# Five second-matmul products of a Strassen MLP get a second level, grown in PSUM

## The chip, the cores and the metric

The kernel runs on 1 core of a Trainium2 chip. The metric is device time in microseconds (us), lower is better. TensorE multiplies into PSUM (8 banks of 128x512 f32), VectorE, ScalarE and GpSimd work beside it, and SyncE (SP) and GpSimd issue the DMAs, each on a queue of its own. Below, one "superblock" is 1024 of the 8192 tokens.

## The reference

```python
# x (8, 1024, 1024), w1 (1024, 4096), w2 (4096, 1024), all float32
h = x @ w1
h = 0.5 * h * (1 + np.tanh(np.sqrt(2 / np.pi) * (h + 0.044715 * h ** 3)))
return (h @ w2).astype(np.float32)
```

## The kernel before

**Tiling.** The 8192 tokens are worked in 8 superblocks of 1024, one after the other; each has a matmul 1 (x by w1, with the gelu) and a matmul 2 (by w2). Operands are float16, sums in PSUM are float32. Both matmuls are split by Strassen's method in Winograd's form: every matrix is cut into four blocks (11, 12, 21, 22), and seven products of sums of blocks take the place of eight products of blocks. The tables `W_SUM` and `S_SUM` (L19, L21) say how an operand sum is made: sum 5 of w2 is block 12 minus block 11, sum 6 is block 22 minus sum 5, and so on; `W_TERM` and `S_TERM` (L18, L20) name the products that take a plain block. The order of the products of matmul 2 in superblocks 0 and 1 is 1, 2, 5, 6, 3, 7, 4.

**One level and two.** A product can itself be done by seven smaller products ("second level", here called steps). Superblocks 0 and 1 run `matmul1` (matmuls L485) and `matmul2_made`, whose products have one level: for each of four token quarters `q`, `matmuls2` (L1059) issues 16 matmuls of 128x512 into one PSUM bank, so 64 in a product. Superblocks 2 to 7 run `matmul1_late` (L699) and `matmul2` (L1018), whose seven products have two levels: 7 steps of 16 matmuls of 128x256, so 112 in a product. The second level needs sums of quarters of both operands. Those of w2 ("inner sums") are made once, by the jobs of `split_jobs`, and stored to the DRAM tensors `in_d[m]`, from which superblocks 2 to 7 load them; the sums of w2 blocks themselves are stored to `w2_d`.

**What happens after a bank.** `post` takes the finished bank of a product and quarter: ScalarE copies it to a temporary (products 1, 5, 6) or VectorE adds it to one (2, 3, 7), and finished outputs are stored over GpSimd's queue. Products that share a letter in the list of `matmul2_made` grow in the same banks ("a", "b", "c").

**Order.** Matmuls, copies, sums and the DMAs issued by `load_in_order` (L158, on SP's queue) keep the order in which the program writes them, engine by engine; each engine takes its queue in that order and stands at an instruction whose data or buffer isn't there. What VectorE does between the products is written by hand in `FILL` (L44 to L58), one table for each of superblocks 0 and 1. The key `61` means after product 6, quarter 1. Its jobs: `g` a sum of gelu outputs (the matmul 2 operand that stands still in TensorE), `w51` piece 1 of w2's sum 5, `p57` the inner sum 7 of product 5's w2 operand, `x`, `q` and `i` sums of the next superblock's x and w1. VectorE's sums all go through `tt` (L135), ScalarE's copies through `act_copy` (L162).

**Memory.** w2 blocks, their sums, inner sums, x blocks and x sums are tiles of the pool `up` (26 buffers, named `u`); stationary sums are tiles of `gcp` (4, named `gc`), float32 temporaries of `tp` (10, `tmp`), PSUM tiles of `pp` (8, `ps`). In `matmul2_made`, `bring` fetches the four pieces of a w2 block (and casts them, in superblock 0), `keep` stores them (superblock 0 only), `x_transpose` fetches the next superblock's x over SP's queue.

Of the kernel before, what the change touches and what calls it, by code (L numbers as in the profile page):

```python
# [14 lines left out]
P = 128  # L15
# [24 lines left out]
def slots(table):  # L40
    return {(int(k[0]), int(k[1])): v.split() for k, v in (row.split(":") for row in table.split(";"))}


FILL = (  # L44
    slots("""10:g60 p15;11:g61 p16;12:g62 p17;13:g63
    ;20:g50 w50 w51;21:g51 w52;22:w53 g52;23:g53 p14
    ;50:w60 w61;51:w62 w63;52:g30 g31;53:g32 g33
    ;60:w70 w71;61:w72 w73;62:w40 w41;63:w42 w43
    ;73:x5;40:x7 x6;41:x3 q5;42:q6 q7 q4
    ;43:i2 i3 i1 i5""".replace("\n    ", "")),  # L50
    slots("""10:g60 w50;11:g61 w51;12:g62 w52;13:g63 w53
    ;20:g50 p55;21:g51 p56;22:g52 p57;23:g53 p54
    ;50:w60 w61;51:w62 w63;52:g30 g31;53:g32 g33
    ;60:p65 w70;61:p66 w71;62:p67 w72;63:p64 w73
    ;30:w40 w41;31:w42 w43;32:p75;33:p76
    ;70:p77 p74;71:x5 p45;72:x7 p46;73:x6 p47
    ;40:p44;41:x3;42:i2;43:i3""".replace("\n    ", "")),
)  # L58
# [13 lines left out]
def kernel(  # L72
# [192 lines left out]
    class StoredHalf:  # L265


        def __init__(self, i, room=()):
            q, h = divmod(i, 2)
            self.ops, self.sums = {}, {}  # L270
            self.room = list(room)
            for ks in GROUPS:
                two = None
                if ks != ("s1", "s5"):
                    two = self.two(ks)
                    if ks == (1, 5):
                        self.both = two
                elif 0 < i < MADE_HALF:
                    two = self.two(ks)
                if two is not None:  # L280
                    nc.sync.dma_start(
                        out=two[:, :len(ks)].rearrange("p e n -> p (e n)"),
                        in_=w1_d[q, ks][:, h].rearrange("p e n -> p (e n)"),
                    )
# [233 lines left out]

    def matmul1(xs, sb, quads, start=None):
        g = g_tiles()  # L520
# [25 lines left out]
        for j in range(NI // 2):  # L546
# [62 lines left out]
            if end:  # L609
                six(0)  # L610
                gelu("11", cs[0], a[0])
                six(1)
                gelu("11", cs[1], a[1])
                for h in range(2):
                    five(h)
# [190 lines left out]

    def matmul2_made(sb, g, keep_w1, xb):

# [30 lines left out]
        def make(m, q):  # L839
            if m not in sums:  # L840
                sums[m] = raw[over[m]] if m in over else [unit(2, HALF) for _ in range(NI // QC)]
            u, op, v = W_SUM[m]
            in0, in1 = (sums[b][q] if isinstance(b, int) else raw[b][q] for b in (u, v))
            tt(sums[m][q], in0, in1, op, True)
            if sb:
                n = 1 if q < 2 else 2
                nc.gpsimd.dma_start(out=w2_at(q, m)[:, :n], in_=sums[m][q][:, :n])

        def pieces(m):
# [4 lines left out]

        s2, a, p5, t6, at = {}, {}, {}, {}, {}
        operands = {1: "11", 2: "12", 4: "22", 7: "21", 5: "11", 3: "12"}
        splits = {m: split_jobs(m, lambda m=m: pieces(m)) for m in (1, *SUMS)}

        def run(key):
            for job in FILL[sb].get(key, ()):  # L860
                kind, m, n = job[0], int(job[1]), int(job[2:] or 0)
                if kind == "g" and m == 6:
                    s2[n] = gcp.tile([P, NI, P], GT, name="gc")
                    tt(s2[n], rows(g["22"], n), rows(g["21"], n), SUB, True)
                elif kind == "g" and m == 5:
                    tt(rows(g["11"], n), s2[n], rows(g["11"], n), ADD, True)
                elif kind == "g":
                    tt(rows(g["12"], n), rows(g["12"], n), s2[n], SUB, True)
                elif kind == "w":
                    make(m, n)  # L870
                elif kind == "p":
                    splits[m][SUMS.index(n)]()
                elif kind == "x":
                    xs.make(m, pin=True)
                elif kind == "q":
                    quad.sum(m, pin=True)
                elif kind == "i" and sb:
                    xs.make_inner(m)
                elif kind == "i":
                    quad.inner_sums(m)  # L880

        def post(m, q, bank):
            if m in (1, 5, 6):
                t = {1: a, 5: p5, 6: t6}[m]
                t[q] = temp()
                act_copy(t[q], bank)
            elif m == 4:
                c = temp()
                act_copy(c, bank)
                store(sb, "21", q, c)  # L890
            else:
                t = {2: a, 3: t6, 7: p5}[m][q]
                tt(t, t, bank, ADD, True)
                at[q] = store(sb, {2: "11", 3: "12", 7: "22"}[m], q, t)

        bring("11", pool_copy, False)
        bring("21", pool_copy, False)
        bring("12", act_copy, True)
        keep("11")
        if sb:  # L900
            bring("22", None, False)
        banks = {"a": [], "b": [], "c": []}
        for m, name, first in (
            (1, "a", True), (2, "b", True), (5, "c", True), (6, "a", False),
            (3, "c", False), (7, "a", False), (4, "a", False),
        ):
            for q in range(NQ):
                if first:
                    banks[name].append(psum())
                bank = banks[name][q]  # L910
                matmuls2(bank, s2[q] if m == 6 else rows(g[operands[m]], q), pieces(m), first)
                post(m, q, bank)
                if (m, q) == (5, 0) and sb == 0:
                    xb = x_cast(sb + 1, nc.gpsimd.tensor_copy(out=pace, in_=p5[0][:, :2]))
                if (m, q) == ((5, 0) if sb else (6, NQ - 1)):
                    xs = XOps(x_transpose(xb, load_in_order))
                    keep("22")
                if (m, q) == (3, NQ - 1) and sb == 0:
                    quad = MadeQuad(0, False, True)
                if (m, q) == (4, 0) and sb:  # L920
                    quad = StoredHalf(0)
                if (m, q) == (1, NQ - 1) and sb == 0:
                    sums[5] = [unit(2, HALF) for _ in range(NI // QC)]
                    for t in sums[5]:
                        act_copy(t[:, 0, :1], warm)
                    bring("22", act_copy, True)
                    keep("21")
                    keep("12")
                run((m, q))
        return xs, [quad]  # L930

    def split_jobs(m, pieces):
        t = {}

# [6 lines left out]
        def make(n):  # L941
            u, op, v = W_SUM[n]
            t[n] = unit(NI // 2, OH // 2)
            for h in range(2):
                tt(t[n][:, h * QC:(h + 1) * QC, :], operand(u, h), operand(v, h), op, True)
            nc.gpsimd.dma_start(out=in_d[m][:, SUMS.index(n)], in_=t[n])

        return [lambda n=n: make(n) for n in SUMS]

    def split_in_m1(m, h):  # L950

        raw, t = [], {}
        for k in range(2):
            raw.append(gcp.tile([P, 2, HALF], DT, name="gc"))
            q = 2 * k + h
            nc.sync.dma_start(out=raw[k], in_=w2_at(q, m))

# [200 lines left out]
    for sb in range(NSB):  # L1158
        if sb < 2:
            g, nxt = matmul1(xs, sb, quads, first if sb == 0 else None)  # L1160
            xs, quads = matmul2_made(sb, g, None if sb else quads[-1].keep_raw, nxt)
            continue
# [33 lines left out]
```

## Time and profile before

| | us |
|---|---|
| median of 3 runs | 1467.45 (1466.58 to 1467.8) |
| the profiled execution: its span (no other time of it is recorded; the median lies 2.55 above) | 1464.9 |
| matmul 2 of superblock 0 (111.94 to 208.63) | 96.69 |
| matmul 1 of superblock 1 (208.63 to 305.32) | 96.69 |
| matmul 2 of superblock 1 (305.32 to 402.01) | 96.69 |
| a later matmul 2 (492.76 to 578.35) | 85.59 |

The span is read from the hardware profile of one execution: first instruction to last. The times of the stages are those of TensorE's unbroken stretches in the chain of work that ended last, on the same clock. In the second matmuls of superblocks 0 and 1, VectorE was busy for 54.70 and 67.84 us, ScalarE for 26.93 and 10.43 and GpSimd for 17.78 and 26.72 (the table by stretches). Over the whole span the DMA engines moved 315 GB/s.

### The profile page before, as it was taken

Reading aid. Unit: us, or ns where it says so; the run is one execution under the profiler, and the core shown is the slowest. Engines: PE = TensorE matmul, PEld = TensorE weight load, DVE = VectorE, ACT = ScalarE, POOL = GpSimd, SP = SyncE. Lnnn points to the kernel's source line nnn. Section 1 sums busy time; section 2 is a strip of 40 time slices with the busy share of each in tenths; the row PEclk is TensorE's granted clock in tenths of the full one; section 3 lists DMA queues with packets and bytes.
Section 4 is the critical chain, followed back from the end, with each engine's and each line's share of the span. In section 5 each row is a group of like instructions: output and inputs, shape, how many; then the busy total and the mean of one; then the engine's idle time right before and its main releaser. Section 6 shows DMA issues by size and latency. Waiting matters only on the chain.

```text
span 1464.9 us, 27508 instructions
## 1 busy us (share of the span) xinstructions
PE 1456.8 (99%) x10383; PEld 1012.9 (69%) x10383; DVE 1166.0 (80%) x1940; ACT 600.7 (41%) x1226; POOL 443.6 (30%) x471
## 2 busy tenths in 40 slices
PE   8999999999999999999999999999999999999998
PEld 5444444444466788668876688767887678866787
DVE  6657459757677899879997799977998779887897
ACT  5665125631066411663126621366214652056410
POOL 1441123312347011560026501274103721136011
PEclk9999999999999999999999999999999999999999
DMA  9999899998998999979999899998999999996896
GB/s 330 342 349 392 229 342 360 385 300 230 353 323 215 360 276 366 375 207 373 307 369 338 203 373 326 359 305 248 350 346 347 297 280 313 352 367 215 310 302 206
DMA packets 207429, 462.15 MB, mean 315 GB/s; under 512 B 75840, under 2 KB 80960, under 8 KB 206400
## 3 DMA queue, kind: packets, MB, share of 16 engines
q1 hardware_dynamic: 179808, 364.96, 72.4%
q0 software_dynamic: 27488, 95.44, 21.9%
q8 instruction: 81, 1.33, 0.3%
q14 instruction: 52, 0.43, 0.1%
HBM read 361.76 MB, written 113.25 MB: 324 GB/s over the span
## 4 chain that ended last, share of the span: by engine, by line
PE 99%; DMA 1%; SPq 0%; DVE 0%; issue 0%; DVEq 0%
PE ps L1018 35%; PE ps L485 31%; PE ps L699 19%; PE ps L1059 13%; PE ps L418 1%; DMA gc<-in_w_dram 1%; SPq L159 0%; PE ps L395 0%; DVE u L223 0%; DVE u L135 0%; DVE u L406 0%; DVEq L135 0%
## 5 line engine op out<-in xcount | busy, mean ns | idle before, releaser
L485 PE MATMUL ps<-u 128*128 128x512 f16 x1808 | 423.5, 379 | 0.0
L135 DVE TENSOR_TENSOR tmp<-tmp,ps 128x512 f32<-128x512 f32 x498 | 280.3, 581 | 106.0 <-PE ps L485 44.6
L162 ACT COPY tmp<-ps 128x512 f32<-128x512 f32 (+1 forms) x398 | 209.4, 545 | 259.4 <-PE ps L1059 135.2
L135 DVE TENSOR_TENSOR ps<-tmp,ps 128x256 f32<-128x256 f32 x552 | 222.7, 425 | 102.9 <-PE ps L699 83.7
L1018 PE MATMUL ps<-u,gc 128*128 128x256 f16 x2688 | 300.3, 273 | 0.0
L485 PEld LDWEIGHTS <-u 128*128 128x128 f16 x1808 | 176.9, 98 | 170.2
L1018 PEld LDWEIGHTS <-gc 128*128 128x128 f16 x2688 | 263.0, 98 | 30.4
L699 PEld LDWEIGHTS <-u 128*128 128x128 f16 x2170 | 212.3, 98 | 67.9 <-issue 0.4
L498 ACT ACTIVATE g<-ps 128x512 f16<-128x512 f32 x326 | 192.9, 596 | 105.3 <-PE ps L699 64.9
L135 DVE TENSOR_TENSOR u<-u 128x2048 f16<-128x2048 f16 (+3 forms) x288 | 214.7, 787 | 23.6 <-DMA w_d<-u 10.9
L1018 PE MATMUL ps<-u,g 128*128 128x256 f16 x2016 | 227.9, 273 | 0.0
L162 ACT COPY u<-ps 128x512 f32<-128x512 f32 (+1 forms) x134 | 78.0, 587 | 354.9 <-PE ps L1018 348.0
L805 POOL DMA_DIRECT2D out_dram<-u x70 | 63.9, 936 | 498.2 <-DVE u L135 264.9
L1018 PEld LDWEIGHTS <-g 128*128 128x128 f16 x2016 | 197.2, 98 | 22.8
L699 PE MATMUL ps<-u 128*128 128x256 f16 x1298 | 193.6, 273 | 0.0
L135 DVE TENSOR_TENSOR u<-u,ps 128x512 f32<-128x512 f32 x216 | 147.7, 684 | 36.5 <-PE ps L1018 25.3
L1059 PE MATMUL ps<-u,g 128*128 128x512 f16 x768 | 166.4, 379 | 0.0
L498 ACT ACTIVATE g<-tmp 128x512 f16<-128x512 f32 x186 | 117.4, 633 | 99.0 <-DVE tmp L135 98.7
L306 POOL TENSOR_TENSOR u<-u 128x512 f16<-128x512 f16 x120 | 136.3, 1157 | 31.8 <-PE ps L699 22.4
L699 PE MATMUL ps<-gc,u 128*128 128x256 f16 x872 | 145.7, 273 | 0.0
L1059 PEld LDWEIGHTS <-g 128*128 128x128 f16 x768 | 75.1, 98 | 90.6
L1012 DVE TENSOR_TENSOR gc<-g,gc 128x2048 f16<-128x2048 f16 x84 | 102.4, 1220 | 3.1 <-PE ps L1018 3.1
(52 smaller groups left out, 854.8 us busy)
## 6 DMA issues: line engine op xcount, KB each, us to landing
u<-w_d SPq DMA_DIRECT2D x322, 512.0 KB, 9.1
u<-in_d SPq DMA_DIRECT2D x168, 512.0 KB, 7.9
out_dram<-u POOLq DMA_DIRECT2D x70, 512.0 KB, 10.8
gc<-in_w_dram SPq DMA_DIRECT2D x48, 512.0 KB, 6.0
g<-w_d SPq DMA_DIRECT2D x40, 512.0 KB, 12.0
w_d<-u POOLq DMA_DIRECT2D x36, 512.0 KB, 7.5
w_d<-u SPq DMA_DIRECT2D x32, 512.0 KB, 9.2
xb<-in_x_dram POOLq DMA_DIRECT2D x56, 256.0 KB, 6.8
```

Of the source, the lines that this page charges most:

```text
L135: i = nc.vector.tensor_tensor(out=out, in0=in0, in1=in1, op=op)
L162: tc.keep_in_program_order(nc.scalar.copy(out=out, in_=in_))
L306: nc.gpsimd.tensor_tensor(out=operand(j), in0=operand(u), in1=operand(v), op=op)
L418: tc.keep_in_program_order(nc.tensor.matmul(bank[:, cols], lhsT=w[:, k, :], rhs=self.xs.blocks[f"{a}{r}"][:, k, cols], start=r == 1 and k ...
L485: tc.keep_in_program_order(nc.tensor.matmul(bank, lhsT=w, rhs=x, start=first and k == 0, stop=k == n - 1, skip_group_check=not first,))
L498: gelu_last[0] = nc.scalar.activation(out=out, in_=src, func=GELU)
L699: tc.keep_in_program_order(nc.tensor.matmul(out, lhsT=w, rhs=x, start=first and k == 0, stop=k == 1, skip_group_check=not first,))
L805: return nc.gpsimd.dma_start(out=rows, in_=src, **kw)
L1012: tc.keep_in_program_order(engine.tensor_tensor(out=self.s[j], in0=in0, in1=in1, op=op))
L1018: tc.keep_in_program_order(nc.tensor.matmul(bank[:, i * OH // 2:(i + 1) * OH // 2], lhsT=t[:, c, i * P:(i + 1) * P], rhs=self.y[j][:, c, : ...
L1059: tc.keep_in_program_order(nc.tensor.matmul(pair(bank), lhsT=a[:, c, :], rhs=chunks(pieces[c // QC])[:, :, c % QC, :], start=(first and c ...
```

## The change

Product 4 of superblock 0 and products 1, 2, 7 and 4 of superblock 1 (the table `DEEP`) get a second level, by the new class `Deep`. It runs its seven steps in the order 1, 5, 6, 2, 7, 3, 4, each in two halves `i` of 128 tokens with 8 matmuls of 128x256, and adds up the steps inside PSUM. Of four banks, two ("upper", `bank(i)`) become the first two token quarters of the product and two ("low", `bank(2 + i)`) the last two. Step 1 goes into low left, and ScalarE copies that to upper left. Step 5 goes into low right, and ScalarE copies that to a temporary. Step 6 adds to low left, and VectorE puts the sum of temporary and low left into upper right. Step 2 adds to upper left. Step 7 adds to low left, and VectorE puts the sum of temporary and low left into low right. Step 3 adds to upper right, step 4 to low left, after which `post` takes the banks.

`Deep.make` (job kind `s` in `FILL`: `s75` is sum 5 for product 7) makes the stationary sums on VectorE, `Deep.load` fetches the stored inner sums over SP's queue. For product 1 of superblock 1 the sums are made by `tail`, called in the last part of that superblock's matmul 1. The `FILL` tables are rewritten: w2's sums 7 and 4 and their inner sums are made in superblock 0, stored over GpSimd's queue; superblock 1 makes sums 5 and 6 and theirs. Sums 5 and 6 are stored over SP's queue (`keep_sum`), as are the inner sums of 6 (`gate`), with the loads of products 2, 7 and 4 behind them on it. In superblock 1 block 12 is fetched before 21 and 22, and the transposes of x are issued after quarter 3 of product 5, not quarter 0. In superblock 0 the block 22 is stored one product earlier (after quarter 3 of product 5, not of 6), ahead of the transposes. Product 4 (and 7 where it is deep, in superblock 1) takes new banks and no longer grows in those of product 1: two float32 tiles of the pool `up` (`half_of`) collect output 21, from products 6, 7 and 4 in superblock 1 and from 7 and 4 in superblock 0. The load of the first stored half of a w1 quad (`StoredHalf(0)`) goes through `load_in_order`.

```diff
+DEEP = ((4,), (1, 2, 7, 4))
+SPLIT_IN_M2 = (7, 4)
+DEEP_STEPS = (1, 5, 6, 2, 7, 3, 4)
 FILL = (
     slots("""10:g60 p15;11:g61 p16;12:g62 p17;13:g63
     ;20:g50 w50 w51;21:g51 w52;22:w53 g52;23:g53 p14
     ;50:w60 w61;51:w62 w63;52:g30 g31;53:g32 g33
-    ;60:w70 w71;61:w72 w73;62:w40 w41;63:w42 w43
-    ;73:x5;40:x7 x6;41:x3 q5;42:q6 q7 q4
-    ;43:i2 i3 i1 i5""".replace("\n    ", "")),
-    slots("""10:g60 w50;11:g61 w51;12:g62 w52;13:g63 w53
-    ;20:g50 p55;21:g51 p56;22:g52 p57;23:g53 p54
+    ;60:w40 w41;61:w42 w43;62:p45 p46;63:p47 p44
+    ;30:w70 w71;31:w72 w73;32:p75 p76;33:p77 s45
+    ;70:p74;71:s47 x5;72:s46;73:s43 x7
+    ;40:x6;41:x3;42:q5;43:q6;44:q7;45:q4;46:i2 i3 i1 i5""".replace("\n    ", "")),
+    slots("""00:w50 w51 w52 w53
+    ;11:s25;12:s27;14:s26;15:s23
+    ;21:g60;22:g61 g50;23:g51;24:g62;25:g63 g52;26:g53
     ;50:w60 w61;51:w62 w63;52:g30 g31;53:g32 g33
-    ;60:p65 w70;61:p66 w71;62:p67 w72;63:p64 w73
-    ;30:w40 w41;31:w42 w43;32:p75;33:p76
-    ;70:p77 p74;71:x5 p45;72:x7 p46;73:x6 p47
-    ;40:p44;41:x3;42:i2;43:i3""".replace("\n    ", "")),
+    ;60:p55 p56;61:p57 p54;62:p65 p66;63:p67 p64
+    ;30:s75;31:s77;32:s76;33:s73
+    ;70:x5;71:x7;72:s45;73:x6;74:s47;75:x3;76:s46
+    ;40:s43;42:i2;43:i3""".replace("\n    ", "")),
 )
 ...
                 gelu("11", cs[1], a[1])
+                if tail is not None:
+                    tail(g)
 ...
+    class Deep:
+        def __init__(self, m, t, pieces, sums=None):
+            self.m, self.pieces = m, pieces
+            self.x, self.s = {b: inner_block(t, b) for b in BLOCKS}, {}
+            self.y = {} if sums is None else sums
+            self.banks, self.copies = {}, {}
+
+        def make(self, j):
+            u, op, v = S_SUM[j]
+            self.s[j] = gcp.tile([P, NI // 2, HT // 2], GT, name="gc")
+            in0, in1 = (self.s[t] if isinstance(t, int) else self.x[t] for t in (u, v))
+            tt(self.s[j], in0, in1, op, True)
+
+        def load(self, steps):
+            for j in steps:
+                self.y[j] = unit(NI // 2, OH // 2)
+                if j in W_TERM:
+                    k, b = (int(d) - 1 for d in W_TERM[j])
+                    load_in_order(
+                        self.y[j].rearrange("p c n -> p (c n)"),
+                        w2_d[k, self.m][:, b].rearrange("p h n -> p (h n)"),
+                    )
+                else:
+                    load_in_order(self.y[j], in_d[self.m][:, SUMS.index(j)])
+
 ...
+        def step(self, j, i):
+            h, cols = {5: (1, right), 2: (0, left), 3: (0, right)}.get(j, (1, left))
+            bank = self.bank(2 * h + i)
+            t = self.x[S_TERM[j]] if j in S_TERM else self.s[j]
+            for c in range(NI // 2):
+                tc.keep_in_program_order(nc.tensor.matmul(
+                    bank[:, cols],
+                    lhsT=t[:, c, i * P:(i + 1) * P],
+                    rhs=self.moving(j, c),
+                    start=(j == 1 and c == 0),
+                    stop=(c == NI // 2 - 1),
+                    skip_group_check=j != 1,
+                ))
+            low = self.banks[2 + i]
+            if j == 1:
+                act_copy(self.bank(i)[:, left], low[:, left])
+            elif j == 5:
+                if not self.copies:
+                    t = temp()
+                    self.copies.update({0: t[:, left], 1: t[:, right]})
+                act_copy(self.copies[i], low[:, right])
+            elif j == 6:
+                tt(self.bank(i)[:, right], self.copies[i], low[:, left], ADD, True)
+            elif j == 7:
+                tt(low[:, right], self.copies[i], low[:, left], ADD, True)
 ...
-            if sb:
+            if sb == 0 and m in SPLIT_IN_M2:
                 n = 1 if q < 2 else 2
                 nc.gpsimd.dma_start(out=w2_at(q, m)[:, :n], in_=sums[m][q][:, :n])
 
+        def keep_sum(m):
+            for q in range(NI // QC):
+                n = 1 if q < 2 else 2
+                load_in_order(w2_at(q, m)[:, :n], sums[m][q][:, :n])
 ...
+        def half_of(q):
+            if q % 2 not in v:
+                v[q % 2] = up.tile([P, 2, OH], F32, name="u")
+            return v[q % 2][:, q // 2, :]
 ...
+                if m == 6 and 7 in deep:
+                    act_copy(half_of(q), bank)
+            elif m == 7:
+                if m in deep:
+                    t = half_of(q)
+                    tt(t, t, bank, ADD, True)
+                    tt(p5[q], p5[q], t, ADD, True)
+                else:
+                    act_copy(half_of(q), bank)
+                    tt(p5[q], p5[q], bank, ADD, True)
+                store(sb, "22", q, p5[q])
             elif m == 4:
-                c = temp()
-                act_copy(c, bank)
-                store(sb, "21", q, c)
+                t = half_of(q)
+                tt(t, t, bank, ADD, True)
+                store(sb, "21", q, t)
             else:
-                t = {2: a, 3: t6, 7: p5}[m][q]
+                t = {2: a, 3: t6}[m][q]
                 tt(t, t, bank, ADD, True)
-                at[q] = store(sb, {2: "11", 3: "12", 7: "22"}[m], q, t)
+                at[q] = store(sb, {2: "11", 3: "12"}[m], q, t)
 
         bring("11", pool_copy, False)
-        bring("21", pool_copy, False)
-        bring("12", act_copy, True)
+        if sb:
+            bring("12", None, True)
+            deep[1].load((5, 6, 7, 4))
+            bring("21", None, False)
+            run((0, 0))
+            keep_sum(5)
+            deep[2].load((5, 6, 7, 4))
+            bring("22", None, False)
+        else:
+            bring("21", pool_copy, False)
+            bring("12", act_copy, True)
         keep("11")
-        if sb:
-            bring("22", None, False)
-        banks = {"a": [], "b": [], "c": []}
+        banks = {"a": [], "c": []}
+
+        def events(m, q):
+            nonlocal xs, xb, quad
+            if sb:
+                if (m, q) == (5, NQ - 1):
+                    keep_sum(6)
+                    deep[7].load(DEEP_STEPS)
+                    xs = XOps(x_transpose(xb, load_in_order))
+                elif (m, q) == (3, 0):
+                    deep[4].load(DEEP_STEPS)
 ...
+            if (m, q) == (5, NQ - 1) and sb == 0:
+                keep("22")
+            if (m, q) == (6, NQ - 1) and sb == 0:
+                xs = XOps(x_transpose(xb, load_in_order))
 ...
+            if (m, q) == (4, 0) and sb:
+                quad = StoredHalf(0, dma=load_in_order)
 ...
+            run((m, q))
+
+        xs = quad = None
         for m, name, first in (
-            (1, "a", True), (2, "b", True), (5, "c", True), (6, "a", False),
-            (3, "c", False), (7, "a", False), (4, "a", False),
+            (1, "a", True), (2, None, True), (5, "c", True), (6, "a", False),
+            (3, "c", False), (7, None if 7 in deep else "a", 7 in deep), (4, None, True),
         ):
+            if m in deep:
+                d = deep[m]
+                for n, j in enumerate(DEEP_STEPS):
+                    for i in range(2):
+                        d.step(j, i)
+                        if j in (3, 4):
+                            post(m, i if j == 3 else 2 + i, d.banks[i if j == 3 else 2 + i])
+                    events(m, n)
+                if name is not None:
+                    banks[name] = [d.banks[q] for q in range(NQ)]
+                continue
             for q in range(NQ):
 ...
-                if (m, q) == ((5, 0) if sb else (6, NQ - 1)):
-                    xs = XOps(x_transpose(xb, load_in_order))
-                    keep("22")
 ...
-            nc.gpsimd.dma_start(out=in_d[m][:, SUMS.index(n)], in_=t[n])
+            if gate:
+                load_in_order(in_d[m][:, SUMS.index(n)], t[n])
+            else:
+                nc.gpsimd.dma_start(out=in_d[m][:, SUMS.index(n)], in_=t[n])
 ...
+            early = []
+
+            def tail(g):
+                early.append(Deep(1, g["11"], None))
+                for n in (5, 7, 6, 3):
+                    early[0].make(n)
+
+            g, nxt = matmul1(xs, sb, quads, first if sb == 0 else None, tail if sb else None)
+            xs, quads = matmul2_made(sb, g, None if sb else quads[-1].keep_raw, nxt, *early)
```

## The prediction

> **What bounds the kernel now.** I read the page first (busy shares, then the chain), then the chain in order of time for the length of each stage, then TensorE's waits, then the single instructions on VectorE around the edited code.
>
> From the page, busy time by engine and the chain by engine:
>
> ```profile
> PE 1456.8 (99%) x10383; PEld 1012.9 (69%) x10383; DVE 1166.0 (80%) x1940; ACT 600.7 (41%) x1226; POOL 443.6 (30%) x471
> ...
> PE 99%; DMA 1%; SPq 0%; DVE 0%; issue 0%; DVEq 0%
> ```
>
> From the chain in order of time (start, length in us), a one-level second matmul (L1059) and a two-level one (L1018), whole:
>
> ```profile
> 305.32 96.69 PE ps L1059 x448
> ...
> 492.76 85.59 PE ps L1018 x784
> ```
>
> TensorE is the chain, without gaps. Seven one-level products take 96.69, so one takes 13.81 (64 matmuls of 0.216). Seven two-level products take 85.59, so one takes 12.23 (112 of 0.109). The two-level stage of the late superblocks runs unbroken, so its matmuls hide their weight loads. TensorE has no wait after the first 12 us. Whatever makes TensorE wait is therefore paid in full, and nothing later can win it back.
>
> VectorE, from its timeline (start, length): a 128x2048 f16 sum behind another, a pair of 128x1024 ones, an add at the end of matmul 1; then the page's row of a 128x256 add in PSUM:
>
> ```profile
> 301.10 0.69 DVE L135 TENSOR_TENSOR tmp<-tmp,ps 128x512 f32<-128x512 f32 x1 [3.01 <-ACT tmp L162]
> 302.82 1.88 DVE L135 TENSOR_TENSOR tmp<-tmp,ps 128x512 f32<-128x512 f32 x3 [1.04 <-PE ps L485]
> ...
> 306.72 1.23 DVE L135 TENSOR_TENSOR gc<-g,g 128x2048 f16<-128x2048 f16 x1
> 307.86 1.22 DVE L135 TENSOR_TENSOR u<-u 128x2048 f16<-128x2048 f16 x1
> ```
> ```profile
> 115.19 1.28 DVE L135 TENSOR_TENSOR u<-u 128x1024 f16<-128x1024 f16 x2
> 116.40 1.21 DVE L135 TENSOR_TENSOR gc<-g,g 128x2048 f16<-128x2048 f16 x1
> ```
> ```profile
> L135 DVE TENSOR_TENSOR ps<-tmp,ps 128x256 f32<-128x256 f32 x552 | 222.7, 425 | 102.9 <-PE ps L699 83.7
> ```
>
> Back to back, then: 1.14 for a 2048-wide sum (a "job" below), 0.605 for a 1024-wide one, 0.6 for a 512-wide add out of PSUM (three in 1.88), 0.43 for a 256-wide add. VectorE is busy 67.84 of the 96.7 us of superblock 1's second matmul (the table by stretches), so there is little room in it.
>
> VectorE also takes its queue in order, and stands still at a wait while later work is ready. Its waits from 140 to 215 us (total, times, longest):
>
> ```profile
> DVE u L135 <- DMA w_d<-u: 10.9, 3, 5.6
> ```
>
> Those were the `w7` sums of superblock 0, held by stores. TensorE did not notice, as no PSUM add that it needed stood behind them.
>
> **The gain.** Five products become two-level: 5 x (13.81 - 12.23) = **7.93 us** less on TensorE.
>
> **What a two-level product needs.** Seven steps of 1.75 us (two halves of 0.87): 1, 5, 6, 2, 7, 3, 4. After each half of 6, VectorE adds into the upper bank that step 2 writes next, so step 2 waits for the add. Only 6's other half (0.87) covers it, and the add takes 0.43: it is free if VectorE is idle at that moment, and every job ahead in its queue is paid by TensorE beyond about 0.4. The operand sums (`s` jobs) must be ready too. So I go through VectorE's queue product by product.
>
> *Superblock 0, product 4.* When product 7 ends, the queue is its last add (0.7), `s43`, `x7`, `x6`, `x3` (4 x 1.14), then the add of step 6: done at 5.8 to 6.2 after the product starts (the two ends use 1.14 and 1.25 a job). Step 2 was due at 5.24: **0.9 lost**. The loads and stores around it move (22 is now kept ahead of the transposes of x), but `x7` comes 8 us after the transposes landed before. Range 0.5 to 3.
>
> *End of matmul 1 in superblock 1.* The four sums of `tail` need the last gelu of g11, which ended at 299.8. Four jobs take VectorE from there to 304.4. The add of p5 that ran at 301.10 runs after them, until 305.1. The last two pieces of matmul 1 (`four`, 0.86 each) write the bank it reads, and were due at 305.2 - 1.7 = 303.5. **1.65 lost**; range 1 to 2.2.
>
> *Product 1.* ScalarE is still busy with the two last gelus 1.7 us into the product; its bank copy (0.38) holds step 5 for **0.35**. VectorE's queue: the g21 difference until 1.3, `w50` to `w53` until 5.85, `s25` until 7.0, then the add of step 6 until 7.4. Step 2 was due at 5.6: **1.8 lost**.
>
> *Product 2.* VectorE is just in time (`g60` ends 0.4 ahead of the add). Its own operands are loaded behind the four stores of sum 5, which wait for `w50` to `w53`: issued 6 to 12 us into product 1 (each also waits for the eighth DMA before it on SP's queue), the first is wanted at 16.2. A load of this kind landed after 9.2 at the median (DMA issues, 300 to 410 us), so 15.5 to 21. I take **0.5**; range 0 to 3.
>
> *Products 5, 6, 3* stay one-level, and their operands are made early enough.
>
> *Product 7 is the point of the change.* Four inner sums of sum 5 (`p55 p56 p57 p54`) stand in VectorE's queue during product 6, ahead of the four of sum 6, the adds of product 3 and the four `s` sums of product 7. Each makes a new tile of the pool `up`, which has 26. When `p57` is due, alive are: 7 loaded operands of product 7, 4 blocks of x, 4 pieces of raw 22, 4 of sum 5, 4 of sum 6, 2 output halves (the second in the place of `p55`), and `p56`. That is 26. Nothing comes free until product 3 has read the first piece of 22 for the last time, 12 matmuls (2.6 us) before its end: in the built program `p57` lies in that piece's place. VectorE stands still from about 43 to 65.6 us after product 1's start, and everything behind `p57` is late. With 0 at the end of product 3:
> - VectorE: twelve halves of p sums from -2.54 to 4.7 (12 x 0.605), an add of product 3, `s75` ready at 6.55. Step 5 was due at 1.75: **4.85 lost**.
> - then add, `s77`, add, `s76`: ready at 10.0. Step 6 was due at 8.35: **1.7 lost**.
> - then add, `s73`, `x5`, `x7`, and the add of step 6: done at 14.4. Step 2 was due at 11.8: **2.6 lost**.
> The other steps run through: the product ends at 21.4 where the old one ended at 13.81. That is 9.2 in all. Bounds: with 0.64 a half (32 took 20.4 in this stage) and 1.25 a job (four in 5.00 at 195.46) it is 10.5; if `x5` and `x7` fall after the add of step 6, 6.9.
>
> *Product 4.* VectorE is still behind: its four pairs of adds, `x3`, `s46` ready at 26.7 on the same clock, step 6 was due at 24.9: **1.85 lost**; range 1 to 3.
>
> *At nothing* I cost these. ScalarE's copies (0.38 and 0.59; it is busy 10.4 of 96.7). The sums that move to superblock 0 (`w4`, `w7`, `p4`, `p7`): 1.8 to 3.4 of each 3.45 us quarter in products 6, 3 and 7. The stores of sums 5 and 6 that go from GpSimd's queue to SP's: past the loads above, the price is in product 2. Product 7's loads: issued 30 us ahead. The transposes of x, now behind them on SP: they took 22 us to issue in superblock 0, and `x5` comes 35 us later. Product 4's loads, on SP behind the stores of sum 6's inner sums and so behind VectorE's hold: issued 12 us ahead, against 9.2 to land; if that cover goes, product 4 waits for the difference.
>
> **Sum.** Given back: 0.9 + 1.65 + 0.35 + 1.8 + 0.5 + 9.2 + 1.85 = 16.25. Less the gain of 7.93: **+8.3**. The profiled span is 1464.9; the median of the runs, 1467.45, lies 2.55 above it. 1464.9 + 8.3 + 2.55 = 1475.8, so **1476**.
>
> **The clock.** TensorE's timeline at the start of the program:
>
> ```profile
> 1.19 3.17 PE L353 MATMUL ps<-idle 128*128 128x512 f16 x7 [1.19 <-DVE warm L1153]
> 5.21 0.62 PE L395 MATMUL ps<-identity,tmp 128*128 128x128 f16 x8 [0.85 <-DVE tmp L387]
> ...
> 12.09 4.49 PE L418 MATMUL ps<-u 128*128 128x512 f16 x20 [0.41 <-DVE u L223]
> ```
>
> The first seven matmuls come 0.43 apart, the twenty later ones 0.216; idle time of 0.85 did not bring the slow pace back. No row has a longer idle time after that. A slow spell as at the start costs 7 x (0.43 - 0.216) = 1.5 us. The Trainium skill (TensorE: Matmul & The Clock Gate, "HAM oscillation — how this bites in real kernels") says that idle time of more than about 3.4 us puts the array back to half clock. By that rule the stall of 4.85 us brings such a spell back, which is the first rival; no row before the change can show it.
>
> **Rivals.**
> 1. *The slow clock comes back* in product 7. One spell, and up to two, at 1.5 each: 1477.5 to 1479. Against it: no row shows the pace fall back once it is up, and the slow steps would partly lie under VectorE's lateness. For it: 4.85 is far over the 0.85 that did no harm. Chance 0.2.
> 2. *VectorE is not held* (a tile is free in time for `p57`), so product 7 costs nothing and product 4 about 0.8. The give-back is 6.0, the gain wins: 1467.45 - 7.93 + 6.0 = 1465.5. It decides if VectorE is through `s76` by 3.5 us into product 7. For it: the slots for `p` jobs fit by duration (2.4 of each 3.45). Against: the count of 26. Chance 0.04.
> 3. *Faster*: the two-level products run as unbroken as in the late superblocks (L1018): 1459.5. It needs VectorE idle at each step 6, which 2048-wide jobs between the steps forbid. Chance 0.04.
> 4. *Only product 7 and 4 stall*, all other give-backs being hidden: 1467.45 - 7.93 + 11.05 = 1470.6 to 1472. Chance 0.07.
> The forecast, 1473 to 1479, has 0.65.
>
> **Numbers.** About 0.2% (2.9 us) is what a measurement of this kernel can tell from no change: under 1464.5 is faster, over 1470.4 slower. Slower: forecast 0.65, rival 1 0.2 and most of rival 4, 0.9. Within: rival 2 and the rest of 4, 0.06. Faster: 0.04. The range goes from rival 4 to the forecast with the loads of product 2 late (+2.5) and a slow spell (+1.5): 1471 to 1480.5.
>
> **What would show it.** In the new trace TensorE's waits should name VectorE, most of them on the second-level line in product 7 of superblock 1, the longest about 4.9; VectorE should be idle for some 20 us in products 6 and 3, ended by TensorE; product 7 should take about 21, products 2 and 4 of superblock 1 about 12.7 and 14, product 1 about 14.4. Superblocks 2 to 7 should be as long as before. I am wrong if VectorE has no such idle time, or if product 7 takes under 14.

## The result and the profile after

The changed kernel took 1502.24 us (median of 4 runs, 1499.61 to 1503.91) against 1467.03 for the kernel before: ratio 1.0238, 95% interval 1.0223 to 1.0253. The forecast of 1476.0 had the sign right and the size wrong: 35 us were lost, not 8. The profiled execution's span is 1501.9, against 1464.9.

The page of the changed kernel, busy time and the chain by engine:

```profile
PE 1456.8 (97%) x10623; PEld 1040.1 (69%) x10623; DVE 1195.1 (80%) x1984; ACT 606.8 (40%) x1246; POOL 436.8 (29%) x459
...
PE 93%; SPq 3%; DVE 1%; DMA 1%; ACT 0%; issue 0%; DVEq 0%
```

TensorE is no longer the whole chain: 3% of the span is SP's sequencer. The chain in order of time says where (start, length):

```profile
168.77 2.49 SPq L164
171.32 16.19 SPq L164
...
219.22 2.93 DMA u<-xb
226.42 9.38 PE ps L857 x64
...
529.70 85.59 PE ps L1159 x784
```

In superblock 0 the chain leaves TensorE from 168.77 on and goes through SP's queue and the transposes of x. The table by stretches (start:end, length, then busy time from TensorE on; the last three are granted clock, DMA share and GB/s) gives the three stages:

```profile
111.94:235.63 123.69, 99.37 (x497) 50.33 (x496) 72.78 (x83) 28.86 (x43) 28.85 (x49) 0.89 1.04 311
235.63:334.22 98.59, 96.86 (x451) 43.84 (x449) 81.97 (x138) 58.38 (x109) 32.14 (x56) 1.00 1.01 369
334.22:438.96 104.74, 92.87 (x642) 63.11 (x641) 72.45 (x97) 16.38 (x35) 9.76 (x18) 0.98 0.86 298
```

Each was 96.69 before. Matmul 2 of superblock 0 is 27.0 longer, matmul 1 of superblock 1 is 1.9 longer and its matmul 2 is 7.9 longer: 36.8 of the span's 37.0. (The last row would give 8.05, but it ends 0.17 late: by TensorE's timeline the next matmul 1 begins at 438.79.) A late matmul 2 is as long as before (85.59). The forecast had -0.7, +1.65 and +7.4 for the three. So the loss in superblock 1 came out as worked out, and superblock 0 is the miss.

There, in product 4 (TensorE's timeline; in brackets the idle time before and who ended it):

```profile
215.01 3.60 PE L857 MATMUL ps<-u,gc 128*128 128x256 f16 x16 [16.50 <-DVE gc L140]
226.42 3.57 PE L857 MATMUL ps<-u,g 128*128 128x256 f16 x16 [7.82 <-DVE ps L140]
```

Such a stretch of 16 takes 1.91 at full pace; from 210 to 230 us the granted clock was 0.50. VectorE's own waits in that time (total, times, longest), and SP's timeline of the 16 transposes before and after:

```profile
DVE u L140 <- DMA u<-xb: 25.5, 2, 19.9
```
```profile
166.22 21.67 SPq L159 DMA_TRANSPOSE u<-xb  x16
```
```profile
168.77 51.71 SPq L164 DMA_TRANSPOSE u<-xb  x16
```

In VectorE's queue `x5` stands ahead of `s46` and `s43`, and `x7` ahead of the add of step 6. They waited for transposes that start 2.6 us later than before and take 30 us longer. What shares the DMA engines with them is in the list of DMA issues (150 to 200 us: operation, count, KB each, median us to landing):

```profile
in_d<-u POOLq DMA_DIRECT2D x8, 512.0 KB, 14.7
w_d<-u SPq DMA_DIRECT2D x5, 512.0 KB, 28.4
...
w_d<-u POOLq DMA_DIRECT2D x4, 512.0 KB, 12.8
w_d<-u POOLq DMA_DIRECT2D x4, 256.0 KB, 11.0
u<-xb SPq DMA_TRANSPOSE x6, 18.1
```

The `in_d` and `w_d` rows on GpSimd's queue are the inner sums and the sums 7 and 4, which the change stores from superblock 0: 8 x 512 + 4 x 512 + 4 x 256 KB, 7 MB. The row on SP is mostly block 22. From 166 to 190 us the DMA engines' share went from 0.70 (161 GB/s) to 1.02 (349 GB/s), by the table by stretches before and after:

```profile
166.00:190.00 24.00, 24.00 (x113) 10.88 (x112) 11.53 (x13) 0.59 (x1) 3.30 (x6) 1.00 0.70 161
```
```profile
166.00:190.00 24.00, 24.00 (x113) 10.90 (x112) 14.02 (x18) 1.53 (x3) 7.14 (x13) 1.00 1.02 349
```

### The profile page after: what moved, and what is told of

Its sections match the earlier page's. It is cut to its first block, busy times and chain, and to the rows that moved or that the text cites. A ratio compares the mean times of both kernels' runs of the same rounds, so it can differ in the third digit from the quotient of the medians.

```text
span 1501.9 us, 28115 instructions
## 1 busy us (share of the span) xinstructions
PE 1456.8 (97%) x10623; PEld 1040.1 (69%) x10623; DVE 1195.1 (80%) x1984; ACT 606.8 (40%) x1246; POOL 436.8 (29%) x459
## 4 chain that ended last, share of the span: by engine, by line
PE 93%; SPq 3%; DVE 1%; DMA 1%; ACT 0%; issue 0%; DVEq 0%
PE ps L1159 34%; PE ps L490 30%; PE ps L706 18%; PE ps L1200 6%; SPq L164 3%; PE ps L857 3%; PE ps L423 1%; DVE u L140 1%; DMA u<-w_d 1%; DMA u<-in_x_dram 0%; PE ps L400 0%; DVE gc L140 0%; DMA u<-xb 0%; DVE tmp L140 0%; ACT g L503 0%
## 5 line engine op out<-in xcount | busy, mean ns | idle before, releaser
L140 DVE TENSOR_TENSOR tmp<-tmp,ps 128x256 f32<-128x256 f32 (+1 forms) x494 | 276.7, 579 | 73.9 <-PE ps L490 42.3
L140 DVE TENSOR_TENSOR ps<-tmp,ps 128x256 f32<-128x256 f32 x572 | 230.7, 425 | 102.3 <-PE ps L706 77.0
L140 DVE TENSOR_TENSOR u<-u 128x512 f32<-128x512 f32 (+3 forms) x280 | 207.6, 782 | 57.4 <-DMA u<-xb 25.5
L167 ACT COPY u<-ps 128x512 f32<-128x512 f32 (+1 forms) x142 | 82.5, 587 | 383.1 <-PE ps L1159 348.5
L1159 PEld LDWEIGHTS <-g 128*128 128x128 f16 x2016 | 197.2, 98 | 22.8
L140 DVE TENSOR_TENSOR u<-u,ps 128x512 f32<-128x512 f32 x228 | 155.6, 683 | 37.4 <-PE ps L1159 27.5
L509 POOL TENSOR_TENSOR g<-g,g 128x1024 f16<-128x1024 f16 x36 | 76.6, 2128 | 93.6 <-ACT g L503 88.6
L1153 DVE TENSOR_TENSOR gc<-g 128x2048 f16<-128x2048 f16 x78 | 95.1, 1219 | 3.4 <-PE ps L1159 3.4
```

What stands on the lines that cost most here:

```text
L140: i = nc.vector.tensor_tensor(out=out, in0=in0, in1=in1, op=op)
L167: tc.keep_in_program_order(nc.scalar.copy(out=out, in_=in_))
L509: tc.keep_in_program_order(engine.tensor_tensor(out=g["21"][:, cs], in0=g["11"][:, cs], in1=g["21"][:, cs], op=SUB,))
L1153: tc.keep_in_program_order(engine.tensor_tensor(out=self.s[j], in0=in0, in1=in1, op=op))
L1159: tc.keep_in_program_order(nc.tensor.matmul(bank[:, i * OH // 2:(i + 1) * OH // 2], lhsT=t[:, c, i * P:(i + 1) * P], rhs=self.y[j][:, c, : ...
```

## The experiments

Theory A: the traffic of these 7 MB slows the transposes. Rival B: the order on SP's queue does (block 22 ahead). Rival C: VectorE's order does (x sums ahead of the stationary ones). Theory D: in superblock 1 the 26 tiles of `up` hold VectorE. Every run was timed beside the kernel before (1466.8 to 1467.0).

**Block 22 behind the transposes.**

```diff
-            if (m, q) == (5, NQ - 1) and sb == 0:
-                keep("22")
             if (m, q) == (6, NQ - 1) and sb == 0:
                 xs = XOps(x_transpose(xb, load_in_order))
+                keep("22")
```

> Only the place of superblock 0's four stores of block 22 on SP's queue is undone: they stand behind the 16 transposes of x again, as before the change. In the changed kernel the transposes took 51.7 us to issue (21.7 before), x5 and x7 waited for them, and TensorE for VectorE (16.5 and 7.8 us in product 4 of superblock 0). Theory A (traffic): what slows the transposes are the stores of w2's sums 7 and 4 and of their inner sums, which GpSimd's queue issues beside them from 159 to 195 us, 7 MB or some 18 us of the DMA engines at 400 GB/s. Then moving 2 MB of 22 helps by a part only: 1490 to 1499. Rival B (order on SP): the slow landing stores of 22 in front of the transposes hold the queue; then the stall is gone: 1473 to 1478.

Measured 1505.03 (ratio 1.0257, 1.0240 to 1.0274). B falls as the whole cause, and A's figure is missed too. The transposes did get faster (42.5 us instead of 51.7), so the order has a part in it. But an inner sum now stood in VectorE's queue for a tile whose store, one of block 22 behind the transposes, had not landed:

```profile
213.94 1.29 DVE L140 TENSOR_TENSOR u<-u 128x1024 f16<-128x1024 f16 x2 [31.69 <-DMA w_d<-u]
```

**The 7 MB behind the transposes, on SP.**

```diff
-                nc.gpsimd.dma_start(out=w2_at(q, m)[:, :n], in_=sums[m][q][:, :n])
+                later(w2_at(q, m)[:, :n], sums[m][q][:, :n])
...
                 xs = XOps(x_transpose(xb, load_in_order))
+                for o, t in held:
+                    load_in_order(o, t)
+                held = None
```

(`later` keeps the DMA in the list `held`, and issues it at once when the list is gone; the inner sums of 7 and 4 in superblock 0 go through it too.)

> The stores of w2's sums 7 and 4 and their inner sums in superblock 0 go over SP's queue behind the 16 transposes instead of over GpSimd's beside them; block 22 stays ahead of the transposes. Theory A: the transposes take about 22 to 30 us, the two waits in product 4 of superblock 0 vanish or shrink under 4 us, and 1474 to 1482 is left, with a new wait of some us possible in matmul 1 of superblock 1, as its first loads of w1 now stand behind 7 MB of stores. Rival B (stores of 22 ahead on SP): the transposes stay slow and the time over 1490.

Measured 1493.29 (1.0182, 1.0167 to 1.0197). The transposes are healed, as A says (24.7 us), with block 22 still ahead of them; the loss is not, and A's figure is missed. SP's transposes, then VectorE's timeline:

```profile
164.65 24.72 SPq L164 DMA_TRANSPOSE u<-xb  x16
```
```profile
207.78 1.22 DVE L140 TENSOR_TENSOR u<-u 128x2048 f16<-128x2048 f16 x1 [17.39 <-DMA in_d<-u]
```

`x5` has its data, but waits for a tile of the pool, and that one holds an inner sum whose store is now late. My expectation had overlooked that stores keep tiles.

**The x sums behind the stationary sums.**

```diff
-    ;70:p74;71:s47 x5;72:s46;73:s43 x7
-    ;40:x6;41:x3;42:q5;43:q6;44:q7;45:q4;46:i2 i3 i1 i5
+    ;70:p74;71:s47;72:s46;73:s43
+    ;43:x5;44:x7 x6;45:x3 q5;46:q6 q7 q4 i2 i3 i1 i5
```

> Superblock 0: the jobs x5, x7, x6, x3 and the q jobs move behind the stationary sums s47, s46, s43 in VectorE's queue (to steps 43 to 46 of product 4); the stores stay. Theory A: the transposes still end about 220 us, as the DMA engines set that; product 4 runs unharmed and the wait moves to the start of matmul 1 in superblock 1, 10 to 16 us instead of 24: 1489 to 1496. Rival C (VectorE's order alone makes the loss): 1473 to 1478.

Measured 1500.57 (1.0228, 1.0213 to 1.0243): C falls, and A's figure is missed. The wait moved on and was paid almost in full, 12.51 of it still in product 4 and 8.22 as late loads of w1 at the start of matmul 1:

```profile
217.95 3.57 PE L857 MATMUL ps<-u,g 128*128 128x256 f16 x16 [12.51 <-DVE ps L140]
229.75 20.43 PE L490 MATMUL ps<-u 128*128 128x512 f16 x84 [8.22 <-DMA u<-w_d]
```

**Without the 7 MB.**

```diff
-                nc.gpsimd.dma_start(out=w2_at(q, m)[:, :n], in_=sums[m][q][:, :n])
+                pass
...
-            else:
+            elif m not in SPLIT_IN_M2:
                 nc.gpsimd.dma_start(out=in_d[m][:, SUMS.index(n)], in_=t[n])
...
+    for m in SPLIT_IN_M2:
+        in_d[m] = in_d[1]
+        for k in range(2):
+            w2_d[k, m] = w2_d[k, 1]
```

> Leaves out the stores of w2's sums 7 and 4 and of their inner sums (7 MB, in superblock 0); who loads them later loads the same number of bytes of product 1's operand instead, so the output is not the reference's. Orders, queues and VectorE's work are those of the changed kernel. Theory A (traffic in superblock 0): the transposes take about 22 to 26 us, TensorE's waits of 16.5 and 7.8 us in product 4 of superblock 0 go to 0.9 to 3, superblock 1 stays as it is: 1474 to 1478. If what slows the transposes is the second level itself or the stores of 22 ahead of them: over 1490.

Measured 1476.43 (1.0067, 1.0052 to 1.0082). SP's transposes and TensorE's wait in product 4 of superblock 0, then its timeline in products 7 and 4 of superblock 1:

```profile
165.92 23.79 SPq L168 DMA_TRANSPOSE u<-xb  x16
```
```profile
201.54 1.91 PE L861 MATMUL ps<-u,g 128*128 128x256 f16 x16 [1.28 <-DVE ps L144]
...
382.13 3.28 PE L861 MATMUL ps<-u,gc 128*128 128x256 f16 x16 [4.80 <-DVE gc L144]
390.06 1.91 PE L861 MATMUL ps<-u,g 128*128 128x256 f16 x16 [2.54 <-DVE ps L144]
...
402.93 1.92 PE L861 MATMUL ps<-u,gc 128*128 128x256 f16 x16 [2.23 <-DVE gc L144]
```

A holds: with the order, the queues of all other DMAs and VectorE's work unchanged, 25.8 us go with the bytes. That the tiles of the left out stores come free sooner here can't be what shortens the transposes: in the run with the stores behind them these tiles were held longer, and the transposes took 24.7. What remains is 9.5 over the kernel before, where 8.3 was forecast.

The same stretch as above shows that the busy share alone would mislead: it is 0.94 here, with 221 GB/s, and the transposes are hardly slower than before.

```profile
166.00:190.00 24.00, 24.00 (x113) 10.87 (x112) 15.12 (x20) 1.75 (x3) 2.96 (x6) 1.00 0.94 221
```

The bytes on GpSimd's queue also slowed the stores that stand ahead of the transposes on SP's. The last of these took, in the list of DMA issues, 24.9 us to land in the changed kernel (issued at 164.64) and 10.8 here (161.86):

```profile
w_d<-u SPq DMA_DIRECT2D x1, 512.0 KB, 24.9
```
```profile
w_d<-u SPq DMA_DIRECT2D x1, 512.0 KB, 10.8
```

**Without the inner sums' 4 MB only.** (The edit of `in_d` from the run above, without that of `w2_d`.)

> Leaves out only the eight stores of the inner sums of 7 and 4 in superblock 0 (4 MB); those of the sums 7 and 4 themselves (3 MB) stay beside the transposes. Who loads the left out sums later loads product 1's inner sums, so the output is not the reference's. All 7 MB out gave 1476.4, none out 1502.2. Theory A, if the loss goes with the bytes: 3 of 7 MB leave some 11 of 25.8 us, 1485 to 1490. If superblock 0 has room for some of it in the stretch from 160 to 190 us, which ran at 150 to 250 GB/s before the change, and only the rest delays the transposes: 1476 to 1482.

Measured 1483.47 (1.0110, 1.0093 to 1.0127), between the two expectations. 3 of the 7 MB leave 7.0 of 25.8 us. The transposes took 33.1 us:

```profile
168.50 33.09 SPq L166 DMA_TRANSPOSE u<-xb  x16
```

So they take 23.8 with no MB, 33.1 with 3 and 51.7 with 7: here every MB lengthens them by 3 to 5 us. Some 2 us of that are hidden (9.3 longer cost 7.0, and 27.9 cost 25.8).

**x fetched later in superblock 1.**

```diff
                     deep[7].load(DEEP_STEPS)
+                elif (m, q) == (6, NQ - 1):
                     xs = XOps(x_transpose(xb, load_in_order))
```

> Superblock 1: the transposes of x are issued after product 6 and not after product 5, so their four tiles of the pool of 26 are not alive when p57 is due; superblock 0 is untouched. Theory D (tiles): VectorE no longer stands still for 22.9 us in products 6 and 3, the four sums of product 7 are ready in time, and product 7 loses under 3 us, not 9.4, unless x5 or x7 (jobs of product 7's first two steps) now wait for the transposes: 1493 to 1498. If the lateness had another cause than the tiles: 1500 to 1504.

Measured 1500.87 (1.0238, 1.0219 to 1.0257). The time is a miss; the mechanism is not. VectorE's hold of 22.9 us is gone and the four sums of product 7 are ready in time. But `x5`, at step 1 of that product, now comes late, and TensorE with it. That it waits for the transposes is read from the times, as VectorE's row names no releaser: the last of them leaves SP at 404.8, and `x5` starts at 408.0. TensorE's row:

```profile
410.88 3.57 PE L857 MATMUL ps<-u,g 128*128 128x256 f16 x16 [6.89 <-DVE ps L140]
```

**And the x sums later.**

```diff
-    ;70:x5;71:x7;72:s45;73:x6;74:s47;75:x3;76:s46
-    ;40:s43;42:i2;43:i3
+    ;72:s45;74:s47;75:x5;76:s46 x7
+    ;40:s43;41:x6;42:x3;43:i2;44:i3
```

> Superblock 1: transposes of x issued after product 6 (as in the run that left 1500.9), and the jobs x5, x7, x6, x3 moved behind the PSUM add of product 7's step 6, most into product 4, as x5 waited for the transposes in that run; superblock 0 untouched. Theory D (tiles, then x): product 7 loses under 2 us of 9.4, product 4 under 2.4: 1491 to 1495. If product 7 is late for VectorE's amount of work and not for its order: no better than 1499.

Measured 1496.79 (1.0207, 1.0190 to 1.0224), 1.8 over the expected range. Product 7 has no wait at all now, so D stands. A third thing came up: product 4's loads, behind the transposes on SP, held TensorE for 3.29, and the matmuls after it ran slow. The four executions spread from 1492.8 to 1498.2, and in the profiled one superblock 0, which the edit leaves alone, was 4.4 shorter than in the changed kernel's. So the gain is better read from superblock 1's matmul 2: 97.9 instead of 104.6.

**Both causes out.** (The edits of the run without the 7 MB and of the two runs above.)

> Both at once: without the stores of sums 7 and 4 and their inner sums (left out, their loads read product 1's operand, so the output is not the reference's), and with the later fetch and sums of x in superblock 1. If the two causes are apart and together the whole of the loss, what is left is the gain of 7.9 us less the waits at the end of matmul 1 and in product 1 of superblock 1 (1.7, 0.4, 1.9) and 1 to 3 us in the two products 4: 1464 to 1468. If they hide each other or a third wait stands behind them: over 1470.

Measured 1469.63 (1.0018, 1.0009 to 1.0028). Above the expectation by 1.6, for that third wait:

```profile
391.17 3.37 PE L861 MATMUL ps<-u,g 128*128 128x256 f16 x16 [3.33 <-DMA u<-w_d]
```

**Both out, product 1 with one level.**

```diff
-DEEP = ((4,), (1, 2, 7, 4))
+DEEP = ((4,), (2, 7, 4))
...
-    ;11:s25;12:s27;14:s26;15:s23
+    ;10:s25;11:s27;12:s26;13:s23
```

(And without `tail` and the loads of product 1's inner sums.)

> The same as the run with both, but product 1 of superblock 1 has one level again: no sums at the end of matmul 1 and no inner sums for it. The prediction said that this product costs more (1.65 + 0.35 + 1.8) than its second level saves (1.59): 2.2 us less than with both, 1462 to 1466. If those waits come back elsewhere (VectorE is as late without them): the time with both, or more by up to 1.6.

Measured 1468.58 (1.0011, 1.0001 to 1.0020), 1.05 better where 2.2 was expected. In the trace matmul 2 of superblock 1 begins 2.1 earlier and its product 1 ends 2.8 earlier (318.90 instead of 321.72), so product 1 does cost more than it saves. Half of that is lost again in product 4, where a longer slow spell follows the same wait (the next 32 matmuls take 4.91, against 3.66 in the run before):

```profile
388.24 3.60 PE L861 MATMUL ps<-u,g 128*128 128x256 f16 x16 [3.22 <-DMA u<-w_d]
```

**Two of product 4's loads ahead of the transposes.**

```diff
                 elif (m, q) == (6, NQ - 1):
+                    deep[4].load((1, 5))
                     xs = XOps(x_transpose(xb, load_in_order))
                 elif (m, q) == (3, 0):
-                    deep[4].load(DEEP_STEPS)
+                    deep[4].load((6, 2, 7, 3, 4))
```

> The run with both changes and one-level product 1 (1468.6), and two of the seven loads of product 4 (steps 1 and 5) go ahead of the transposes on SP's queue; the stores of sums 7 and 4 and their inner sums in superblock 0 are left out here too, so the output is not the reference's. In that run TensorE's longest wait, 3.2 us, was for the first load of product 4, which stood behind the 16 transposes, and some 3 us of slow clock came after it. Theory: both go, 1462 to 1465. If the loads only move the wait to the other five or take a tile that p57 or p64 needs: 1467 to 1472.

Measured 1468.20 (1.0010, 1.0000 to 1.0019): no gain. The wait for the load is gone, and VectorE's lateness after product 7 (eight adds, `x5`, `s46`) stood right behind it:

```profile
391.79 2.59 PE L861 MATMUL ps<-u,gc 128*128 128x256 f16 x16 [2.23 <-DVE gc L144]
395.53 3.57 PE L861 MATMUL ps<-u,g 128*128 128x256 f16 x16 [1.15 <-DVE ps L144]
```

**One part alone, and a version without the causes.** Superblock 0's product 4 alone, its inner sums made in place and not stored, the sums 7 and 4 stored in superblock 1 as before:

```diff
-DEEP = ((4,), (1, 2, 7, 4))
+DEEP = ((4,), ())
...
-    ;30:w70 w71;31:w72 w73;32:p75 p76;33:p77 s45
-    ;70:p74;71:s47 x5;72:s46;73:s43 x7
-    ;40:x6;41:x3;42:q5;43:q6;44:q7;45:q4;46:i2 i3 i1 i5
+    ;30:w70 w71;31:w72 w73;33:s45
+    ;71:s47 x5;72:s46;73:s43 x7
+    ;40:x6;42:x3 q5;43:q6;44:q7;45:q4;46:i2 i3 i1 i5
```

> One part alone: only product 4 of superblock 0 has the second level, its inner sums made in place and not stored there; superblock 1 has the jobs, loads and stores of the kernel before. If the second level itself is sound and only the stores beside it cost: 1.59 less 0 to 1.3 under the kernel before, 1465.3 to 1467. If making p4 in superblock 0 or the two more tiles for output 21 hold the transposes or x5: over 1468.

The same with product 2 of superblock 1, whose inner sums superblock 1's matmul 1 has stored in any case (`DEEP = ((4,), (2,))`, its `s` jobs in product 1, the `p5` jobs moved from product 2 to 6):

> Only two products get the second level: 4 in superblock 0, with its inner sums made in place and not stored there, and 2 in superblock 1, whose inner sums lie in DRAM already. Sums 7 and 4 and their inner sums are stored in superblock 1 as before the change, so superblock 0 gets no more DMA traffic; x3 stands behind the PSUM add of step 6 in superblock 0. By theory A superblock 0 keeps its whole gain of 1.6 but for 0 to 1.3, and product 2 cost nothing but its 12.2 us in the runs so far: 2 x 1.59 less 0 to 1.5 is 1.7 to 3.2 us under the kernel before: 1463.5 to 1466. If VectorE, now with four more sums and eight more adds in superblock 1, is late in product 6, 3 or 7: 1467 or more.

The first took 1465.76 (0.9993, 0.9984 to 1.0002), not told from no change; the second 1465.15 (0.9987, 0.9978 to 0.9996), a little faster than the kernel before: its slowest execution (1465.74) lies below the fastest of that kernel (1466.61). Its only waits of TensorE are those of the start, and its two deep products stand without a gap in the chain in order of time:

```profile
194.99 5.24 PE ps L856 x48
200.25 7.15 PE ps L856 x64
...
317.91 6.18 PE ps L856 x56
324.09 6.27 PE ps L856 x56
```

Products 4 and 2 take 12.4 each where 13.81 stood. That is 2.8 in all; the profiled span is 1.8 shorter, as what follows the last matmul 2 took 1.0 longer in this execution.

## Why the prediction was wrong

**The step that failed** is the cost of the sums that move to superblock 0, put "at nothing", with "1.8 to 3.4 of each 3.45 us quarter". That priced VectorE's time. The sums 7 and 4 were in fact made in superblock 0 before, too (`w70` to `w43` in its table); new there are their inner sums, and the stores of both. These 16 stores, 7 MB on GpSimd's queue, were not in the sum. By an estimate they keep the 16 DMA engines busy for some 18 us, at the 401 GB/s of the stretch from 125.8 to 139.6 us before the change, and the stretch where the engines were least busy (0.70) was where the transposes of x ran. So the term for product 4 of superblock 0, 0.9 with a range of 0.5 to 3, rested on transposes landing as before. Its cover was "`x7` comes 8 us after the transposes landed before", and they took 30 us longer. It measured 28.6: 27.0 longer, and its gain of 1.59. The two waits are 24.3 of it, TensorE's slow pace behind them 4.0 (3.60, 3.57 and 4.26 where 1.91, 1.91 and 3.66 are usual). The run without these stores puts the wait at 1.28 and the whole at 1476.4.

**What held**, measured against forecast: the end of matmul 1 in superblock 1 1.73 (1.65); product 1 0.25 and 1.78 (0.35 and 1.8); product 2 nothing (0.5, range from 0); product 7 4.81, 0.25 and 2.55 (4.85, 1.7 and 2.6), the second smaller, most likely because TensorE ran slow just before it; product 4 2.23 (1.85). Product 7 as a whole took 21.6 (21.4). VectorE stood still for 22.9 us (22.6 forecast), ended by TensorE:

```profile
400.14 7.31 DVE L140 TENSOR_TENSOR u<-u 128x1024 f16<-128x1024 f16 x12 [22.93 <-PE ps L1200]
```

The run that fetches x later shows that tiles were the reason: with four fewer alive, VectorE's longest wait in products 6 and 3 is 5.1, and product 7's sums are in time. One small term was off: the 2.55 from the span to the median held some spread of the runs, and in the changed kernel the profiled execution's time lies 1.8 above its span (1503.69 and 1501.9).

**The clock**, the first rival, was real but small beside the rest. After the wait of 4.81, 16 matmuls took 3.21 instead of 1.91, 1.3 us; the forecast priced a spell at 1.5. As the prediction said of this rival, part of it lay under VectorE's lateness: the next wait was 0.25, where 1.7 was forecast. In product 4 of superblock 0 the slow pace cost the 4.0 above.

**The covers** of the prediction were the weak part. It named that of product 4's loads ("if that cover goes, product 4 waits for the difference"), and it went as soon as product 7 was mended. That a store also holds its tile until it lands, the prediction had read in the kernel before (the `w7` sums, 10.9 us), but it was not carried into the sum; two runs paid 17 and 32 us for it.

## What to carry to other kernels

When work is moved to another stage, move every DMA that it issues in the sum too, and set the bytes against the stretch where they fall, not against the average of the span. Look at what else runs in that stretch: a transfer on another queue that a late engine needs soon pays for it. Where tiles are scarce, sending stores later heals the transfer and starves the pool, so order alone could not win the time back; the version that gained moved no stores into superblock 0.

## What the runs showed of the hardware

The transposes on SP's queue took 21.7 us for 16 with the DMA engines at 0.70, and 51.7 beside 7 MB of stores from GpSimd's queue. The Trainium skill (Trainium Kernel Development and Optimization, "Key Constraints") says that DMAs of all queues run on the same 16 engines and interleave; by that rule the two queues are no protection from each other, and the runs with 0, 3 and 7 MB agree.

Plain stores ahead of the transposes on SP's own queue seem to be part of it. The second transpose alone stood on SP for 16.2 us in the changed kernel, until 187.5, and the last store ahead of it landed at 189.5. Without the 7 MB these two times are 170.4 and 172.6, with 3 MB 177.2 and 180.1, with the 7 MB behind the transposes 170.3 and 173.0, and with block 22 behind them 174.2 and 177.4: each time the transpose was through 2.0 to 3.2 us before that store landed. No run tests this by itself.

TensorE's pace fell to half after an idle time of 16.50 (3.60 for 16 matmuls instead of 1.91), after 3.33 (3.37) and 3.22 (3.60), not after 2.55 or 1.78. After 2.23 it held in the changed kernel (1.92) and fell in another run (2.59, then 3.57 behind 1.15 more). And in the run with block 22 behind the transposes it held after 3.67:

```profile
229.90 1.91 PE L857 MATMUL ps<-u,g 128*128 128x256 f16 x16 [3.67 <-DVE ps L140]
```

The page TensorE: Matmul & The Clock Gate of the Trainium skill, in "HAM oscillation — how this bites in real kernels", puts the limit at some 3.4 us of idle time; the runs here show half pace below it and full pace above it. So no single limit comes out of them, and what else decides was not tested.
